# A two-buffer ring for the down phase's raw blocks, five held blocks, recurrence tiles allocated early, more gate tiles

## The chip, the cores and the metric

The kernel runs on one core of one Trainium2 chip. The metric is the device time of one execution in microseconds; the median of three runs of the kernel before is 3393.79 us (3392.86 to 3396.34).

## What is computed

One encoder layer on 1024 + 256 tokens (`x_prompt`, `x_sample`), D = 1024, feed-forward width 2816, in float32. The reference, cut to what matters:

```python
def swiglu(h, w_gate, w_up, w_down):
    return (jax.nn.silu(h @ w_gate) * (h @ w_up)) @ w_down

h = rms_norm(x, norm_g[0])
x = x + 0.5 * rms_norm(swiglu(h, ffn_w_gate[0], ...), norm_g[1])
h = rms_norm(x, norm_g[2])
p = h @ w_in
p_rw, p_att, p_gate = _split(p, [RWKV_COLS, ATT_COLS, GATE_COLS])
y_a = rwkv7_bidir(p_rw, ...)          # 8 heads x 64, both directions
y_b = axial_gqa(p_att, qk_norm_g)     # 8 query heads, 2 key heads
g_a, g_b = _split(sigmoid(p_gate + b_gate), [D_MODEL, D_MODEL])
merged = g_a * (y_a @ w_branch_a) + g_b * (y_b @ w_branch_b)
x = x + rms_norm(merged @ w_out, norm_g[3])
h = rms_norm(x, norm_g[4])
x = x + 0.5 * rms_norm(swiglu(h, ffn_w_gate[1], ...), norm_g[5])
```

## The kernel before, in words

Every operand of a float32 matmul is split into a high and a low half (`split`, L115 on ACT makes the high half, L116 on VectorE the low one), and a product is three matmuls: high by high, high by low, low by high. The stages follow one another: first feed-forward network (from the start to 878 us), projections and attention with gates, the preparation of the recurrence, the recurrence (1742 to 2296 us) with branch b between its steps, branch a, the output projection, the second feed-forward network, the end.

**Feed-forward.** `gate_up` makes 11 pairs of hidden columns. At the end of a pair it writes seven combinations of the two (`A11` to `A22`, `S1` to `S4`) to the DRAM tensor `a_d` (L360), four combinations of the down weights to `t_d` (L352). `down` then multiplies by one level of Strassen-Winograd: `DOWN` lists four banks X, Y, Z, V with 2, 1, 2 and 2 products, each over 11 blocks, so 77 blocks. A block (L393 to L404) is a load of 128x640 from `a_d` into a raw tile `sraw` (L395), its split into `S`, a load of 128x512 (`traw`, L400 or L403) from `t_d` or the weights `wd`, and its split. `mm` (L406) does the 3 matmuls for one of five token tiles, so a block is 15 matmuls. In the banks X, Y and Z, `S` is one of six slots of a tile `sr`; in bank V it is a tile `sS` of the ring `t5`, which has three buffers. The raw tiles come from the ring `x1` (two buffers) for the first two blocks and from `sc` (six buffers) after that; `sc` is also used by `gate_up` until its last column. The last `LAST` = 3 blocks of bank V are held: their matmuls are done token tile by token tile, so that tile 0 is finished while the others still run. `done` (L411) combines the banks, `half` (L377) squares and scales, `end` (L381) adds the residual and writes the row; `after` starts the next norm and, after the first network, the transposes (L176, L180, L181) which the projections (L140) read.

**Recurrence.** `loop_consts` (L685) allocates its constants and eight tiles `AR`, which are cleared before use, four on VectorE and four on POOL (L708), and two early tiles `bk0`. The pools it gets are `ep` and `cp`; `ep` lies in memory that is free during the preparation. `fetch` (L894) loads `AR` and `BK` per step, `g` (L920) multiplies them, L927 on VectorE masks the result with `gm`, POOL writes it to `Bm`, and the inverse (L959) follows.

**Branches.** `branch` (L1410) multiplies the recurrence's or the attention's output, five chunks of 256 tokens (`yr`, `yT`), by eight weight tiles (`pbr`, L1427), multiplies by a gate tile `g` loaded from `gate_d` (L1430, L1431), and, in branch a, `emit_m` adds branch b's tile `mb` (L1470, L1471) and splits the sum for the output projection (`po`, L1513). `NGA` = 6 is the number of `g` buffers in branch a, and `m` has three.

The order of the instructions on each engine is the scheduler's, by data dependences and by the buffers of the rings; all DMAs of these stages are issued from SP, whose queue is in order.

Of the kernel before, what the change touches and what calls it, by code (L numbers as in the profile page):

```python
# [7 lines left out]
F32 = mybir.dt.float32  # L8
F32R = mybir.dt.float32r
# [26 lines left out]
NH = NF // 2  # L36
TH = TT // 2
HT = NT // 2
LAST = 3

AB7 = ("A11", "A12", "S2", "S1", "S4", "S3", "A22")
DOWN = (("X", (("A11", "B11"), ("A12", "B21"))), ("Y", (("S2", "T2"),)), ("Z", (("S1", "T1"), ("S4", "B22"))),
# [7 lines left out]
class K:  # L50
# [311 lines left out]
    def down(self, W, WY, st, ps, wd, a_d, t_d, gb, xres, put, after):  # L362

        nc = self.nc

        sr = self.hp.tile([128, 6, 2, HT], F32R, name="sr", tag="h512")
        uv = self.hp.tile([128, 3, TH, 512], F32, name="uv", tag="h512")
        u, p5, v = (uv[:, i] for i in range(3))
        xr = self.hp.tile([128, 4, D], F32, name="xr", tag="h256")
        s2 = WY.tile([128, TT, 2], F32, name="s2")  # L370
        ys = [None] * TT
        lo, hi = slice(0, 512), slice(512, 1024)

        def half(t, h, src):

            hs = (lo, hi)[h]
            y = ys[t][:, hs]  # L377
            nc.scalar.activation(out=self.junk[:, :512], in_=src, func=AF.Square, accum_out=s2[:, t, h:h + 1])
            nc.vector.tensor_tensor(out=y, in0=src, in1=gb[:, hs], op=ALU.mult)

        def end(t):  # L381
            x = xr[:, t % 4]
            nc.sync.dma_start(out=x, in_=xres(t))
            ss = st.tile([128, 1], F32, name="ss")
            nc.vector.tensor_tensor(out=ss, in0=s2[:, t, 0:1], in1=s2[:, t, 1:2], op=ALU.add)
            sd = st.tile([128, 1], F32, name="sd")
            nc.scalar.activation(out=sd, in_=ss, func=AF.Sqrt, scale=4.0 / D, bias=self.eps4)
            r = st.tile([128, 1], F32, name="r")
            nc.vector.reciprocal(r, sd)
            nc.vector.scalar_tensor_tensor(out=ys[t], in0=ys[t], scalar=r, in1=x, op0=ALU.mult, op1=ALU.add)  # L390
            nc.sync.dma_start(out=put(t), in_=ys[t])

        def block(n, small, sn, tn, f):  # L393
            raw = W.tile([128, HT], F32, name="sraw", tag="x1" if n < 2 else "sc")
            nc.sync.dma_start(out=raw, in_=a_d[AB7.index(sn), f])  # L395
            S = W.tile([128, 2, HT], F32R, name="sS", tag="t5") if small else sr[:, n % 6]
            self.split(S[:, 0], S[:, 1], raw)
            raw = W.tile([128, 512], F32, name="traw", tag="w2")
            if tn[0] == "T":
                nc.sync.dma_start(out=raw, in_=t_d[int(tn[1]) - 1, f])  # L400
            else:
                fb, c = f + NH * (tn[1] == "2"), 512 * (tn[2] == "2")
                nc.sync.dma_start(out=raw, in_=wd[fb * 128:fb * 128 + 128, c:c + 512])  # L403
            return S, self.opr(raw)  # L404

        def mm(p, i, S, T, first, last):  # L406
            ts = slice(i * 128, i * 128 + 128)
            for m, (x, y) in enumerate(((0, 0), (0, 1), (1, 0))):
                nc.tensor.matmul(p, lhsT=S[:, x, ts], rhs=T[:, y], start=first and m == 0, stop=last and m == 2, skip_group_check=True)  # L409

        def done(bank, second, i, p):  # L411
            t, w = i, TH + i
            if bank == "X" and not second:
                nc.scalar.copy(u[:, i], p)
            elif bank == "X":
                ys[t] = WY.tile([128, D], F32, name="y", tag="y")
                half(t, 0, p)
            elif bank == "Y":
                nc.vector.tensor_tensor(out=u[:, i], in0=u[:, i], in1=p, op=ALU.add)
            elif bank == "Z" and not second:  # L420
                nc.scalar.copy(p5[:, i], p)
            elif bank == "Z":
                y = ys[t][:, hi]
                nc.vector.tensor_tensor(out=y, in0=u[:, i], in1=p, op=ALU.add)
                half(t, 1, y)
                end(t)
            elif not second:
                ys[w] = WY.tile([128, D], F32, name="y", tag="y")
                y = ys[w][:, hi]
                nc.vector.tensor_tensor(out=v[:, i], in0=u[:, i], in1=p, op=ALU.add)  # L430
                nc.vector.tensor_tensor(out=y, in0=v[:, i], in1=p5[:, i], op=ALU.add)
                half(w, 1, y)
            else:
                y = ys[w][:, lo]
                nc.vector.tensor_tensor(out=y, in0=u[:, i], in1=p, op=ALU.add)
                half(w, 0, y)
                end(w)
        n = 0
        for bank, prods in DOWN:
            bk = [ps.tile([128, 512], F32, name="pd", tag="mm") for _ in range(TH)]  # L440
            for j, (sn, tn) in enumerate(prods):
                final = bank == "V" and j == 1
                kept = []
                for f in range(NH):
                    S, T = block(n, bank == "V", sn, tn, f)
                    n += 1
                    if final and f >= NH - LAST:
                        kept.append((f, S, T))
                        continue
                    for i in range(TH):  # L450
                        mm(bk[i], i, S, T, j == f == 0, f == NH - 1)
                        if f == NH - 1:
                            done(bank, j, i, bk[i])

                for i in range(TH if kept else 0):
                    for f, S, T in kept:
                        mm(bk[i], i, S, T, False, f == NH - 1)
                    done(bank, j, i, bk[i])
                    after(TH + i, ys)
                if j == len(prods) - 1 - (bank == "V"):  # L460
                    after(bank, ys)
# [143 lines left out]
       "TT": 7, "tt": 9, "y1": 6, "zs": 2, "Sn": 3, "SP": 2}  # L605
RPB = {"i": 4, "g": 1, "z": 1, "s": 1}
NGD = 5
NGA = 6
WFB = {}
Y4 = 2  # L610
D4 = 8
# [9 lines left out]
class Rwkv:  # L621
# [63 lines left out]
    def loop_consts(self, ep, cp):  # L685

        nc, I, kk = self.nc, self.k.I, self.k
        self.gm = ep.tile([128, 4, 128], F32, name="gm")
        nc.sync.dma_start(out=self.gm, in_=I["c_gm"].rearrange("p (u t) -> p u t", u=4))
        self.lv = cp.tile([128, 6, 128], F32, name="lv")  # L690
        nc.sync.dma_start(out=self.lv, in_=I["c_lv"].rearrange("p (u t) -> p u t", u=6))
        self.e64 = cp.tile([128, 64], F32, name="e64")
        nc.vector.tensor_copy(self.e64[:64], kk.ident[:64, :64])
        nc.vector.tensor_copy(self.e64[64:], kk.ident[64:, 64:])
        self.Bm, self.Bl = [], []
        for i in range(self.NB):
            bm = cp.tile([128, 2, 128], F16, name=f"Bm{i}")
            bl = cp.tile([128, 2, 128], F16, name=f"Bl{i}")
            nc.gpsimd.memset(bm, 0.0)
            nc.gpsimd.memset(bl, 0.0)  # L700
            self.Bm.append(bm)
            self.Bl.append(bl)
        self.bk0 = [ep.tile([128, 4, 2, 64], F32, name=f"BK{i}") for i in range(2)]
        self.step_no = 0
        self.AR = []
        for i in range(self.NAR):
            ar = (ep if i < 2 else cp).tile([128, 4, 2, 2, 64], F32, name=f"AR{i}")
            (nc.vector if i < 4 else nc.gpsimd).memset(ar, 0.0)  # L708
            self.AR.append(ar)
        self.ar_no = 0  # L710

    def pad_tile(self, W):
# [182 lines left out]
    def fetch(self, pp, segs, W, out):  # L895

        nc, q = self.nc, pp["q"]
        for d, (sg, early) in enumerate(segs):
            cc = slice(4 * sg, 4 * sg + 4)
            AR = self.AR[self.ar_no % len(self.AR)]  # L900
            self.ar_no += 1
            for h in range(2):
                hs = slice(64 * h, 64 * h + 64)
                nc.sync.dma_start(out=AR[hs, :, h], in_=self.xs["ar"][q, d][hs, cc])
            BK = self.bk0.pop() if self.bk0 else W.tile([128, 4, 2, 64], F32, name="BK", tag="BK")
            nc.sync.dma_start(out=BK, in_=self.xs["bk"][q, d][:, cc])
            out[d] = (AR, BK)

# [393 lines left out]
def build(tc, I, O):  # L1302
    nc = tc.nc
    k = K(tc, I, O)
    with tc.tile_pool(name="cst", bufs=1) as cp, tc.tile_pool(name="dr", bufs=1, space=DRAM) as dr, \
# [14 lines left out]
        with tc.tile_pool(name="hp", bufs=1, side="right") as hp, tc.tile_pool(name="wp", bufs=2, side="right") as k.wp:  # L1320
# [3 lines left out]
            with tc.tile_pool(name="W", bufs=1, side="right") as W0, tc.tile_pool(name="ps", bufs=1, space=PSUM) as ps:  # L1324
                W, ps = Bufs(W0, FB), Bufs(ps, FP)
# [52 lines left out]
            with tc.tile_pool(name="vp", bufs=1) as vp:  # L1378
                Vt = vp.tile([128, TT, 2, 2, 64], F32R, name="Vt", tag="Vt")

                with tc.tile_pool(name="W", bufs=1) as W0, tc.tile_pool(name="ps", bufs=1, space=PSUM) as ps:
                    W = Bufs(W0, {"t5": 3, "act": 2, "pad": 3})
# [64 lines left out]
        with tc.tile_pool(name="hp", bufs=1) as hp:  # L1447
            k.hp = Bufs(hp, {"h512": 2, "h256": 1})
            mT = [k.htile(ci) for ci in range(3)]
            with right:  # L1450
# [12 lines left out]
                        pass  # L1463
                early.close()
                with tc.tile_pool(name="W", bufs=1) as W0, tc.tile_pool(name="ps", bufs=4, space=PSUM) as ps:
                    W = Bufs(W0, {"g": NGA, "m": 3})

                    def emit_m(dt, ci, c0, n, g):
                        mb = W.tile([128, n], F32, name="mb", tag="m")
# [16 lines left out]
                    first = out_w(right.enter_context(tc.tile_pool(name="wo", bufs=1, side="right")), 0)  # L1486
# [110 lines left out]
```

## Time and profile before

| what | value |
|---|---|
| median of three runs | 3393.79 us |
| profiled execution, its own time | 3395.69 us |
| its span | 3393.9 us |
| mean granted clock of TensorE | 0.986 |
| TensorE busy | 3268.3 us, 96% |
| VectorE busy | 2106.7 us, 62% |
| ACT busy | 1559.1 us, 46% |
| DMA, mean over the span | 128 GB/s |

A row of a timeline is a merged run of equal instructions: start, duration from first start to last end, engine, line, operation, tiles, count, and in brackets how long the engine stood idle before it and what released it. A row of waits names who waited for whom, the total, the number of times and the longest. A row of stretches gives busy time by engine, then TensorE's granted clock (1.00 is full speed), the share of the DMA engines and what they moved. "to landing" is the time from a DMA's issue to the arrival of its data.

### The profile page before, as it was taken

The page shows a single profiled execution, that of the slowest core. Times are in us where ns is not written, and L with a number is a line of the kernel's source. Part 1 is how long each engine was busy: PE and PEld are TensorE (multiplying, and loading weights), DVE is VectorE, ACT ScalarE, POOL GpSimd, SP SyncE. Part 2 cuts the span into 40 slices and gives each one's busy share as a digit, 9 for nine tenths or more (in the row PEclk, how much of TensorE's full clock was granted, in tenths as well). Part 3 has the DMA queues.
Part 4 walks back from the last instruction along what each step waited for, and adds up shares of the span by engine and source line. Part 5 has one row for each costly group of instructions (what it writes and reads, how often), then busy time and mean ns, then how long its engine had stood idle before and what let it go on. Part 6 is the DMA issues. An engine that isn't in the chain of part 4 may idle for free.

```text
span 3393.9 us, 57823 instructions
## 1 busy us (share of the span) xinstructions
PE 3268.3 (96%) x21750; PEld 2738.1 (81%) x21750; DVE 2106.7 (62%) x4047; ACT 1559.1 (46%) x3048; POOL 333.4 (10%) x695
## 2 busy tenths in 40 slices
PE   7999999999899999999979999998999999999998
PEld 6888888788778888887767888888777888887887
DVE  7665665456446767648867676655548656656446
ACT  6322223345325666746646666652444223233434
POOL 0000000000011000012234444420000000000000
PEclk9999999999999999999999999999999999999999
DMA  4343344756234121224353222127523433436655
GB/s 145 132 143 123 125 142 135 243 174 205 84 97 132 57 65 57 73 92 151 133 168 103 60 75 74 46 73 227 183 80 118 141 118 129 138 118 210 196 165 183
DMA packets 255640, 433.64 MB, mean 128 GB/s; under 512 B 28032, under 2 KB 109184, under 8 KB 255232
## 3 DMA queue, kind: packets, MB, share of 16 engines
q1 hardware_dynamic: 255360, 429.95, 38.9%
q8 instruction: 171, 2.80, 0.4%
q14 instruction: 109, 0.89, 0.1%
HBM read 278.97 MB, written 147.59 MB: 126 GB/s over the span
## 4 chain that ended last, share of the span: by engine, by line
PE 41%; DMA 3%; DVE 3%; ACT 1%; issue 1%; POOL 1%; SPq 0%; DVEq 0%; POOLq 0%; ACTq 0%
PE pd L409 8%; PE Z L258 4%; PE V L258 4%; PE T L258 4%; PE X L258 3%; PE po L1513 3%; PE g L920 2%; PE Y L258 2%; PE inv L959 2%; PE inv L964 2%; PE inv L965 1%; PE zu L996 1%; PE zu L1000 1%; PE zu L1007 1%; PE yp L1022 1%; PE sp L1015 1%
## 5 line engine op out<-in xcount | busy, mean ns | idle before, releaser
L140 PE MATMUL pp<-hT,whi 128*128 128x512 f32 (+1 forms) x1776 | 503.6, 363 | 8.3 <-ACT qk L1194 5.3
L115 ACT CAST op<-w 128x512 fp32r<-128x512 f32 x356 | 220.6, 623 | 513.5 <-PE V L258 122.2
L409 PE MATMUL pd<-op,sr 128*128 128x512 f32 x1650 | 384.0, 395 | 8.5 <-ACT sr L115 8.5
L409 PEld LDWEIGHTS pd<-op,sr 128*128 128x128 f32 x1650 | 312.2, 189 | 80.0 <-ACT sr L115 9.4
L116 DVE TENSOR_TENSOR op<-w,op 128x512 fp32r<-128x512 f32 x356 | 243.0, 689 | 185.1 <-ACT op L115 184.6
L140 PEld LDWEIGHTS pp<-hT,whi 128*128 128x128 f32 x1776 | 315.7, 192 | 48.0 <-ACT qk L1194 6.1
L140 PE MATMUL pp<-hT,wlo 128*128 128x512 f32 (+1 forms) x888 | 320.6, 361 | 0.0
L258 PEld LDWEIGHTS T<-hT,op 128*128 128x128 f32 x2112 | 275.3, 193 | 24.3 <-DVE op L116 10.5
L258 PE MATMUL T<-hT,op 128*128 128x256 f32 x2112 | 280.6, 286 | 10.7 <-DVE op L116 9.6
L258 PE MATMUL X<-hA,op 128*128 128x512 f32 x1056 | 263.2, 397 | 6.5 <-DVE op L116 3.3
L967 ACT CAST tt<-inv 128x512 f16<-128x512 f32 x400 | 226.3, 589 | 91.7 <-PE inv L965 69.1
L258 PEld LDWEIGHTS X<-hA,op 128*128 128x128 f32 x1056 | 196.3, 190 | 50.1 <-DVE op L116 4.4
L961 DVE TENSOR_TENSOR y<-inv,lv 128x256 f16<-128x256 f32 x400 | 162.1, 419 | 84.0 <-PE inv L959 61.0
L116 DVE TENSOR_TENSOR sr<-sraw,sr 128x640 fp32r<-128x640 f32 x110 | 90.6, 825 | 172.8 <-ACT sr L115 172.7
L140 PEld LDWEIGHTS pp<-hT,wlo 128*128 128x128 f32 x888 | 170.1, 192 | 18.7
L115 ACT CAST sr<-sraw 128x640 fp32r<-128x640 f32 x110 | 80.0, 729 | 185.5 <-PE pd L409 176.2
L409 PE MATMUL pd<-op,sS 128*128 128x512 f32 x660 | 152.2, 391 | 0.0
L1427 PE MATMUL pbr<-yT,whi 128*128 128x256 f32 x640 | 127.4, 298 | 22.9 <-ACT yT L115 8.4
L258 PE MATMUL V<-hX,op 128*128 128x512 f32 x528 | 144.7, 395 | 0.0
L409 PEld LDWEIGHTS pd<-op,sS 128*128 128x128 f32 x660 | 123.3, 188 | 25.9 <-DVE sS L116 0.6
L258 PE MATMUL Z<-hB,op 128*128 128x512 f32 x528 | 137.3, 394 | 0.0
L964 PE MATMUL inv<-y,tt 128*128 128x128 f16 x800 | 130.1, 220 | 0.0
(315 smaller groups left out, 6730.2 us busy)
## 6 DMA issues: line engine op xcount, KB each, us to landing
sraw<-a_d SPq DMA_DIRECT2D x154, 320.0 KB, 3.2
w<-wgu SPq DMA_DIRECT2D x192, 256.0 KB, 3.3
a_d<-sg SPq DMA_DIRECT2D x88, 320.0 KB, 2.6
w<-wd SPq DMA_DIRECT2D x88, 256.0 KB, 2.8
t_d<-w SPq DMA_DIRECT2D x88, 256.0 KB, 2.8
traw<-t_d SPq DMA_DIRECT2D x88, 256.0 KB, 3.1
a_d<-s SPq DMA_DIRECT2D x66, 320.0 KB, 2.3
traw<-wd SPq DMA_DIRECT2D x66, 256.0 KB, 3.6
```

The costliest lines, as they stand in the source:

```text
L115: self.nc.scalar.copy(dst_h, src)
L116: self.nc.vector.tensor_tensor(out=dst_l, in0=src, in1=dst_h.bitcast(F32), op=ALU.subtract)
L140: nc.tensor.matmul(p[:, :n], lhsT=a[:, ks], rhs=h[:, b, k], start=i == 0, stop=i == 23)
L258: self.nc.tensor.matmul(out, lhsT=o[:, a, ks], rhs=rhs(k, b), start=start and i == 0, stop=stop and i == 11, skip_group_check=True)
L409: nc.tensor.matmul(p, lhsT=S[:, x, ts], rhs=T[:, y], start=first and m == 0, stop=last and m == 2, skip_group_check=True)
L920: nc.tensor.matmul(g[:, 2 * d:2 * d + 2], lhsT=BK[:, cs[d] % 4], rhs=AR[:, cs[d] % 4], start=True, stop=True)
L959: nc.tensor.matmul(m[:, h], lhsT=Bm[:, h], rhs=tt[:, h, 0], start=True, stop=True)
L961: nc.vector.tensor_tensor(out=y1, in0=m, in1=mask(l), op=ALU.mult)
L964: nc.tensor.matmul(dbl[:, h, 0], lhsT=tt[:, h, 1], rhs=y1[:, h], start=True, stop=True)
L967: nc.scalar.copy(tt, dbl)
L1427: nc.tensor.matmul(p, lhsT=a[:, ks], rhs=ys[ci][:, b, kk], start=i == 0, stop=i == 11)
L1513: nc.tensor.matmul(p, lhsT=m[:, a, kk, mo:mo + 128], rhs=wo[hf][:, b, kk], start=i == 0, stop=i == 23)
```

## The change

Four things are done. In `down`, raw tiles of the first five blocks and of all blocks of bank V come from `x1`; the others from `sc` as before. In bank V the split block is a `t5` tile (three buffers) for odd blocks and a pair of `sc` tiles (three pairs) for even ones, and `LAST` is 5. In `loop_consts` the `AR` tiles are allocated directly behind `gm`, ahead of the other constants, and cleared at the end as before; the tiles `bk0` are gone, and all `BK` come from the ring. In branch a `g` has ten buffers and `m` five.

```diff
@@ -36,7 +36,7 @@
-LAST = 3
+LAST = 5
@@ -391,10 +391,18 @@
         def block(n, small, sn, tn, f):
-            raw = W.tile([128, HT], F32, name="sraw", tag="x1" if n < 2 else "sc")
+
+            raw = W.tile([128, HT], F32, name="sraw", tag="x1" if n < 5 or small else "sc")
             nc.sync.dma_start(out=raw, in_=a_d[AB7.index(sn), f])
-            S = W.tile([128, 2, HT], F32R, name="sS", tag="t5") if small else sr[:, n % 6]
-            self.split(S[:, 0], S[:, 1], raw)
+            if not small:
+                S = sr[:, n % 6]
+                S = (S[:, 0], S[:, 1])
+            elif n % 2:
+                S = W.tile([128, 2, HT], F32R, name="sS", tag="t5")
+                S = (S[:, 0], S[:, 1])
+            else:
+                S = [W.tile([128, HT], F32R, name="sH", tag="sc") for _ in range(2)]
+            self.split(S[0], S[1], raw)
@@ -605,7 +613,7 @@
-NGA = 6
+NGA = 10
@@ -687,6 +695,8 @@
         nc.sync.dma_start(out=self.gm, in_=I["c_gm"].rearrange("p (u t) -> p u t", u=4))
+
+        self.AR = [(ep if i < 2 else cp).tile([128, 4, 2, 2, 64], F32, name=f"AR{i}") for i in range(self.NAR)]
         self.lv = cp.tile([128, 6, 128], F32, name="lv")
@@ -700,13 +710,9 @@
-        self.bk0 = [ep.tile([128, 4, 2, 64], F32, name=f"BK{i}") for i in range(2)]
         self.step_no = 0
-        self.AR = []
-        for i in range(self.NAR):
-            ar = (ep if i < 2 else cp).tile([128, 4, 2, 2, 64], F32, name=f"AR{i}")
+        for i, ar in enumerate(self.AR):
             (nc.vector if i < 4 else nc.gpsimd).memset(ar, 0.0)
-            self.AR.append(ar)
         self.ar_no = 0
@@ -902,7 +908,7 @@
-            BK = self.bk0.pop() if self.bk0 else W.tile([128, 4, 2, 64], F32, name="BK", tag="BK")
+            BK = W.tile([128, 4, 2, 64], F32, name="BK", tag="BK")
@@ -1463,7 +1469,7 @@
-                    W = Bufs(W0, {"g": NGA, "m": 3})
+                    W = Bufs(W0, {"g": NGA, "m": 5})
```

The changed order on the engines, at three places. The first is SP at the start of the first down phase, from the second block's load on, before:

```order
L395 DMA sraw<-a_d 128x640
L403 DMA traw<-wd 128x512 x5
L360 DMA a_d<-sg 128x640 x2
L360 DMA a_d<-s_4998 128x640
L360 DMA a_d<-s_4999 128x640
L360 DMA a_d<-sg 128x640 x2
L360 DMA a_d<-s_5000 128x640
L534 DMA gb<-ng 128x1024
L395 DMA sraw<-a_d 128x640 x11
```

and now, from the third block's load on:

```order
L396 DMA sraw<-a_d 128x640
L411 DMA traw<-wd 128x512
L396 DMA sraw<-a_d 128x640
L411 DMA traw<-wd 128x512
L383 DMA xr<-x_prompt 128x1024
L360 DMA a_d<-sg 128x640 x2
L360 DMA a_d<-s_4998 128x640
L360 DMA a_d<-sg 128x640 x2
L360 DMA a_d<-s_4999 128x640
L360 DMA a_d<-s_5000 128x640
L542 DMA gb<-ng 128x1024
L396 DMA sraw<-a_d 128x640 x8
```

The loads of blocks 2 and 3 and one `xr` now stand ahead of the seven writes of the last column and of `gb`; block 4's is the first behind them.

The second is VectorE at the entry to the recurrence, from the low half of branch b's first weight tile on, before:

```order
L113 SCALAR_TENSOR_TENSOR wlo<-wraw,whi 128x512
L693 COPY e_15945<-ident 64x64
L694 COPY e_15945<-ident 64x64
L708 MEMSET AR_15978 128x1024
L708 MEMSET AR_15980 128x1024
L708 MEMSET AR_15982 128x1024
L708 MEMSET AR_15984 128x1024
L116 TENSOR_TENSOR yT<-yr,yT 128x1024
L1431 SCALAR_TENSOR_TENSOR g<-g,pbr 128x256
L927 TENSOR_TENSOR gs<-g,gm 128x512
```

and now:

```order
L113 SCALAR_TENSOR_TENSOR wlo<-wraw,whi 128x512
L703 COPY e_15964<-ident 64x64
L704 COPY e_15964<-ident 64x64
L715 MEMSET AR_15956 128x1024
L715 MEMSET AR_15957 128x1024
L116 TENSOR_TENSOR yT<-yr,yT 128x1024
L933 TENSOR_TENSOR gs<-g,gm 128x512
```

Two of the four clears have moved ahead, among the preparation's operations, and the mask of the first `g` product comes before the first gate product.

The third is SP in branch a, from the fourth of its five loads of `yr` on (the numbers tell buffers apart), before:

```order
L1416 DMA yr_26630<-ya_d_75 128x4x256
L1430 DMA g_26652<-gate_d_71 128x256
L1416 DMA yr_26635<-ya_d_75 128x4x256
L1470 DMA mb_26655<-mb_d_74 128x256
L1430 DMA g_26673<-gate_d_71 128x256
L1470 DMA mb_26676<-mb_d_74 128x256
L1430 DMA g_26694<-gate_d_71 128x256
L1470 DMA mb_26697<-mb_d_74 128x256
L1430 DMA g_26715<-gate_d_71 128x256
L1470 DMA mb_26718<-mb_d_74 128x256
L1430 DMA g_26736<-gate_d_71 128x256
L124 DMA wraw_26747<-wba 128x512
```

and now:

```order
L1422 DMA yr_26641<-ya_d_75 128x4x256
L124 DMA wraw_26758<-wba 128x512
L1422 DMA yr_26646<-ya_d_75 128x4x256
L1436 DMA g_26663<-gate_d_71 128x256
L1476 DMA mb_26666<-mb_d_74 128x256
L1436 DMA g_26684<-gate_d_71 128x256
```

The second weight tile's load has moved from behind five gate loads to ahead of the fifth `yr`, and the first gate load from ahead of the fifth `yr` to behind it.

## Rows read from the trace of the kernel before

**Rows 1.** The page: busy time by engine.

```profile
PE 3268.3 (96%) x21750; PEld 2738.1 (81%) x21750; DVE 2106.7 (62%) x4047; ACT 1559.1 (46%) x3048; POOL 333.4 (10%) x695
```

**Rows 2.** Timeline of PE, start of the first and the second down phase.

```profile
601.42 7.00 PE L409 MATMUL pd<-op,sr 128*128 128x512 f32 x30
612.83 7.36 PE L409 MATMUL pd<-op,sr 128*128 128x512 f32 x25 [4.41 <-ACT sr L115]
...
3121.57 8.65 PE L409 MATMUL pd<-op,sr 128*128 128x512 f32 x30 [4.13 <-ACT sr L115]
```

**Rows 3.** Timeline of all engines from 604 us, first down phase.

```profile
603.97 0.82 DVE L358 TENSOR_TENSOR s<-sg,s 128x640 f32<-128x640 f32 x1
604.82 0.32 SPq L360 DMA_DIRECT2D a_d<-s  x1
...
605.70 11.58 SPq L395 DMA_DIRECT2D sraw<-a_d  x11
...
612.05 4.03 ACT L115 CAST sr<-sraw 128x640 fp32r<-128x640 f32 x5 [2.98 <-DMA sraw<-a_d]
```

**Rows 4.** The tile sraw, 593 to 620 us: low-half split, time to landing.

```profile
L116 DVE TENSOR_TENSOR sr<-sraw,sr x7: 817/826/826, 612.8 to 620.0; 128x640 fp32r<-128x640 f32 x7
...
DMA to landing us min/median/max: 3.3/6.3/7.1
```

**Rows 5.** Busy time and clock of three stretches behind waits: columns as described above.

```profile
612.83:615.83 3.00, 3.00 (x7) 2.42 (x8) 2.97 (x4) 2.67 (x4) 0.00 (x0) 0.51 0.96 346
...
3121.57:3124.57 3.00, 3.00 (x7) 2.42 (x8) 2.99 (x4) 2.65 (x4) 0.00 (x0) 0.50 0.93 328
...
2351.20:2355.00 3.80, 3.80 (x18) 3.80 (x19) 1.75 (x5) 0.57 (x2) 0.00 (x0) 0.50 0.78 227
```

**Rows 6.** The tile sraw, 780 to 870 us (bank V): time to landing.

```profile
DMA to landing us min/median/max: 2.8/3.5/5.3
```

**Rows 7.** Timelines of DVE and PE, end of the first down phase.

```profile
872.23 1.28 DVE L390 SCALAR_TENSOR_TENSOR y<-y,r,xr 128x1024 f32<-128x1024 f32 x1
...
877.05 1.28 DVE L390 SCALAR_TENSOR_TENSOR y<-y,r,xr 128x1024 f32<-128x1024 f32 x1
...
876.72 1.40 PE L409 MATMUL pd<-op,sS 128*128 128x512 f32 x5
...
906.72 0.73 PE L140 MATMUL pp<-hT,whi 128*128 128x512 f32 x2 [1.08 <-DVE hT L181]
```

**Rows 8.** Timelines of PE and DVE, end of the kernel.

```profile
3361.68 22.76 PE L409 MATMUL pd<-op,sS 128*128 128x512 f32 x99
...
3389.14 1.28 DVE L390 SCALAR_TENSOR_TENSOR y<-y,r,xr 128x1024 f32<-128x1024 f32 x1
```

**Rows 9.** Waits of PE, 1730 to 1760 us.

```profile
PE pbr L1427 <- ACT yT L115: 7.2, 1, 7.2
PE inv L959 <- DVE tt L955: 3.7, 2, 1.9
PE pbr L1427 <- DVE yT L116: 3.2, 1, 3.2
```

**Rows 10.** Timelines of DVE and SP, entry to the recurrence.

```profile
1739.79 0.91 DVE L708 MEMSET AR<- 128x1024 f32 x1 [0.26 <-issue]
...
1743.96 1.22 DVE L116 TENSOR_TENSOR yT<-yr,yT 128x1024 fp32r<-128x1024 f32 x1
...
1740.73 1.25 SPq L904 DMA_DIRECT2D AR<-ar_d  x2
```

**Rows 11.** Waits of PE and of DVE in branch a and around it.

```profile
PE pbr L1427 <- DVE g L1431: 5.2, 5, 2.4
PE po L1513 <- DVE g L1431: 3.1, 1, 3.1
PE pbr L1427 <- ACT whi L112: 2.5, 1, 2.5
...
DVE g L1431 <- DMA g<-gate_d: 16.7, 13, 3.4
```

More of the change, by code (lines that the diff above doesn't have):

```diff
@@ L408, in mm @@
             for m, (x, y) in enumerate(((0, 0), (0, 1), (1, 0))):
-                nc.tensor.matmul(p, lhsT=S[:, x, ts], rhs=T[:, y], start=first and m == 0, stop=last and m == 2, skip_group_check=True)
+                nc.tensor.matmul(p, lhsT=S[x][:, ts], rhs=T[:, y], start=first and m == 0, stop=last and m == 2, skip_group_check=True)
         def done(bank, second, i, p):
```

## Prediction

> **What bounds the kernel now.** I read the page first, for the engines' shares; then TensorE's own timeline, for the places where it stands still; then, at each of them, the waits and the queue of the engine that releases it; and the table by stretches, for the clock after each. TensorE is busy for 3268.3 us of a span of 3393.9 us [rows 1], so the path is TensorE nearly everywhere, and only its idle time and the time in which it runs at half clock can be won. The change takes no matmul away and adds none. Its five parts touch five places; each is costed against the profiled execution, whose time (3395.69 us) is 1.9 us above the median of the runs shown (3393.79 us). I take the same saving off the median.
>
> **Start of each down phase.** Down is 77 blocks of 15 matmuls. TensorE runs two of them, 30 matmuls in 7.00 us (with the overlap of neighbours some 3.4 us a block), then stands still for 4.41 us in the first feed-forward network and for 4.13 us in the second, waiting for the ACT half of block 2's split [rows 2]. The reader should see why that is late: block 2's load is on SP behind the writes of the last feed-forward column and the broadcast of `gb`; the last of those writes waits for a VectorE operation of 0.82 us, and the load itself is issued at 605.70 only [rows 3]. Loads issued there take 6.3 us to land, 7.1 at most [rows 4]: 605.70 and 6.3 is 612.0, ACT's split starts at 612.05 [rows 3] and TensorE at 612.83 [rows 2].
> The gap costs more than its length. In the 3.0 us behind it the granted clock is 0.51 in one phase and 0.50 in the other, the level of 1.2 GHz, and 7 matmuls are done [rows 5]. At the rate of rows 2 (30 in 7.00 us, 0.23 us each) they would need 1.6 us: 1.4 us lost. Together 4.41 + 4.13 + 2 x 1.4 = 11.3 us.
> The Trainium skill ("TensorE: Matmul & The Clock Gate", "Loop structure matters more than you think") states as a rule that a long wait for a transfer between matmuls leaves TensorE at the lower clock when it goes on. By that rule the gaps alone, 8.5 us, would be too little, and the trace agrees [rows 5].
> With the change blocks 0 to 3 are loaded ahead of these writes, since ring `x1` gives a buffer back when a block is split. Two more splits of 0.82 us on VectorE [rows 4] come ahead of the operations that the writes wait for, so the writes and `gb` go out 1.6 us later: block 4's load is issued near 607.3, lands near 613.6, and ACT's split (five in 4.03 us, 0.8 us each [rows 3]) ends near 614.4. TensorE, without its gap, wants block 4 at 601.42 + 4 x 3.4 = 615.0. VectorE's half is needed two matmuls later (615.5) and ends near 615.3. It just fits; with a landing of 7.1 us it is late by some 0.7 us. I take 0.3 us a phase: **10.7 us**, with bounds 7.3 (2 us late in each, the clock kept) and 11.3. The two extra splits hide beside TensorE's first blocks; the load of `xr` that moves ahead of the writes is one of the transfers that land beside those two blocks.
> A page would price the landing otherwise: the Trainium skill ("DMA: Bandwidth & Descriptors", "Anatomy of one DMA") fits 2.0 us and the bytes at 436 GB/s, measured on another issuing path, which makes 2.75 us for 320 KB. By that estimate block 4 comes 3.6 us earlier and the term would be the full 11.3; rows 4 say 6.3 in this place, and go into the sum.
>
> **Five blocks held, six buffers for them.** In the last product the five held blocks are run tile by tile: 15 matmuls a tile instead of 9, 3.4 us instead of 2.04. The first tile is done at P - 13.6 instead of P - 8.2, P being the end of the phase on TensorE. No matmul moves in or out.
> After the first phase a chain follows (VectorE, ACT, VectorE, for each tile: combine, square, scale, root, residual, then the next norm). Its residual additions come 4.8 us apart (872.23, 877.05) though TensorE gives a tile each 2.04, so TensorE waits for it, and the projections start at 906.72, 28.6 us after P = 876.72 + 1.40 = 878.1 [rows 7]. An earlier first tile moves this chain earlier by up to 5.4 us. But in the new order VectorE also takes splits of weights and the copies of the next transposes between the tiles, and the tiles now come at 3.4 us each, 13.6 us for the last four. Laid out by hand with the durations of rows 7 the projections start at P + 27, so I take **2.0 us**, from -1 (the transposes, which TensorE takes in order, wait for a tile between the held matmuls) to +6.
> At the end of the kernel the five tiles go one after the other on VectorE, from P - 13.6, with an estimated 4.1 us each: 1.28 for the addition [rows 8], 0.7 each for combining, squaring and scaling, which are half as large, and 0.7 for the root's three small steps; the fourth and fifth end at P + 1.4 and P + 5.6. Before, the last addition ended at 3390.42, 6.0 us after P = 3384.44 [rows 8]. **0.3 us**, 0 to 0.6.
>
> **Entry to the recurrence.** TensorE waits 7.2 us for the high half of `yT` and then 3.2 us for the low one [rows 9]. The first wait is for loads of weights and `yr`, which stay. The second is VectorE's: four clears of `AR`, from 1739.79 on, stand ahead of that split at 1743.96, 1.04 us each [rows 10]. Two of them move into the preparation, so the split starts 2.1 us earlier. SP also drops five loads of some 0.6 us from the train that ends with the `BK`s [rows 10], and the first `g` products come ahead of most of the `pbr` products, which then fill two waits for `tt` of 3.7 us together [rows 9]. From 2.1 (the clears alone) to 5.8 (both waits filled too). I take **3.5 us**, nearer the middle, since the chain through POOL between them stays. The two clears in the preparation take some 2 us of VectorE there while TensorE works; if that cover is gone they cost 0.5 at most. The low clock behind the first wait stays.
>
> **Branch a.** TensorE waits there 5.2 us for the products with `g` and 2.5 us for `whi` [rows 11], and runs at half clock behind the latter [rows 5]. The new order issues the second weight tile ahead of the fifth `yr`, which removes the 2.5 us and, with it, about 1.9 us of low clock (half of the 3.8 us [rows 5]). Against this: the first `g` and `mb` now go behind the last `yr`, and VectorE has a backlog at the branch's end: `po` waits 3.1 us for it [rows 11]. Ten buffers let loads run ahead, but they don't make VectorE faster. I take **2.5 us**, from -1 (the late `g` costs what the weights give) to +6 (most of both waits).
>
> **Sum.** 10.7 + 2.0 + 0.3 + 3.5 + 2.5 = 19.0 us, so 3375 us from the median of 3393.79. With all lower bounds the saving is 7.3 - 1 + 0 + 2.1 - 1 = 7.4 us (3386), with all upper ones 11.3 + 6 + 0.6 + 5.8 + 6 = 29.7 us (3364).
>
> **Rivals.**
> *The gap moves to block 4.* If SP stands at block 2's load until block 0 is split, the writes behind it are late by more than the two splits. At 3 us late, block 4 is a new gap of 3 us with its 1.4 us of low clock: the starts give 11.3 - 8.8 = 2.5, the whole 10.8, the time 3383 us. For it: VectorE is in order, and busy with the writes' operands [rows 3]. Against it: blocks 0 and 1 were split without stopping the queue, since TensorE had them at 601.42.
> *The chains shift whole.* The transition gives 5.4 us and branch a loses all its waits, 6 us: 26 us, 3368 us. For it: the wait on `gate_d` is VectorE's longest, 16.7 us [rows 11]. Against it: the wait of `po`, which is VectorE's work and no load's.
> *Two raw buffers starve the last bank (slower).* The 22 blocks of bank V load through a ring of two instead of six. A slot turns in the landing plus 1.6 us of splits plus 0.3 of issue, so a block can come every (landing + 1.9) / 2: at 3.5 us, the median there [rows 6], 2.7 us, less than the 3.4 of a block. It decides above 4.9 us of landing for many blocks in a row. If the 6.3 us of rows 4 held there, 4.1 us a block, 0.7 late, times 44 blocks is 31 us, and with 19 saved the time is 3406 us. Against it: the median, and the six buffers for splits.
>
> **How the numbers follow.** A measurement of this kernel tells 0.2%, 6.8 us, from no change. The forecast has 0.70, the gap at block 4 0.12, the whole shift 0.10, the starved bank 0.03; 0.05 is left for parts that cancel, near 3390. The range is 3364 to 3388 us: all bounds of the unknown costs, the first two rivals, and 2 us for the last case. Faster by over 0.2% comes from the forecast but for its edge and from the first two rivals: 0.88; same 0.08; slower 0.04.
>
> **What would show it.** In the new profile: 75 matmuls without a stop from the start of each down phase and a clock of 1.00 there; block 4's split by ACT just before TensorE comes to it; the first tile of the last product 13.6 us before the phase's end, projections some 27 us after it; the low half of `yT` two clears earlier and the first `g` product soon behind; no wait for `whi` in branch a. Wrong would be: a stop at block 4 or 5 of more than 2 us, waits for `sS` or `sH` through bank V, or a longer wait of `po`.

## The result and the profile after

The changed kernel takes 3375.28 us (median of four runs, 3374.04 to 3376.69) against 3394.53 us: a ratio of 0.9943, 95% interval 0.9926 to 0.9961. That is 19.2 us less; 19.0 was forecast. The profiled execution has a span of 3373.8 us. Two later sets of runs gave 0.9940 (0.9925 to 0.9955) and 0.9943 (0.9929 to 0.9956).

The page of the changed kernel, by engine (before: [rows 1]):

```profile
PE 3268.5 (97%) x21750; PEld 2742.1 (81%) x21750; DVE 2101.1 (62%) x4047; ACT 1556.8 (46%) x3048; POOL 332.1 (10%) x695
```

TensorE's work is the same; what went is time in which it stood still or ran at half clock. The starts of the two down phases, TensorE's timeline of the changed kernel (before: [rows 2]):

```profile
598.78 26.50 PE L417 MATMUL pd<-op,sr 128*128 128x512 f32 x116
...
3104.70 25.46 PE L417 MATMUL pd<-op,sr 128*128 128x512 f32 x108
```

and the busy time and clock of both starts, with the columns of [rows 5]:

```profile
600.00:616.00 16.00, 16.00 (x72) 13.27 (x71) 10.01 (x16) 6.46 (x11) 0.00 (x0) 1.00 1.00 334
...
3110.00:3125.00 15.00, 15.00 (x66) 12.08 (x65) 9.50 (x15) 7.93 (x13) 0.00 (x0) 1.00 1.00 359
```

The row of each start is whole, no bracket interrupts it, and the clock is 1.00 where it was 0.51 and 0.50. Why it is whole, in the queue of SP and in ACT's timeline of the changed kernel:

```profile
594.18 0.33 SPq L396 DMA_DIRECT2D sraw<-a_d  x1
...
597.79 0.80 SPq L360 DMA_DIRECT2D a_d<-sg  x2
...
604.01 0.40 SPq L542 DMA_DIRECT2D gb<-ng  x1
604.46 8.91 SPq L396 DMA_DIRECT2D sraw<-a_d  x8
...
610.10 0.73 ACT L115 CAST sr<-sraw 128x640 fp32r<-128x640 f32 x1 [3.65 <-DMA sraw<-a_d]
```

Block 3's load is issued at 594.18, ahead of the first write at 597.79. Block 4's follows `gb` at 604.46 and its data release ACT at 610.10, 5.6 us later; TensorE, which began at 598.78, comes to it 13.6 us after that, at 612.4. So 1.6 us are to spare after ACT's 0.73. In the second phase of the same profile the margin is smaller:

```profile
3101.92 4.53 SPq L396 DMA_DIRECT2D sraw<-a_d  x7
...
3107.92 0.73 ACT L115 CAST sr<-sraw 128x640 fp32r<-128x640 f32 x1 [4.74 <-DMA sraw<-a_d]
```

There the load takes 6.0 us, and TensorE comes to block 4 at 3109.39, 0.7 us after the end of ACT's split. Over the sixteen starts of the eight profiles with this edit, the load of block 4 took 5.2 to 7.1 us and the margin was 0.6 to 2.3 us; TensorE stopped at block 4 in none.

The transition behind the first phase (before: [rows 7]), timelines of VectorE and TensorE of the changed kernel:

```profile
857.54 1.28 DVE L390 SCALAR_TENSOR_TENSOR y<-y,r,xr 128x1024 f32<-128x1024 f32 x1
...
862.51 1.28 DVE L390 SCALAR_TENSOR_TENSOR y<-y,r,xr 128x1024 f32<-128x1024 f32 x1
...
867.34 1.28 DVE L390 SCALAR_TENSOR_TENSOR y<-y,r,xr 128x1024 f32<-128x1024 f32 x1
...
873.83 1.28 DVE L390 SCALAR_TENSOR_TENSOR y<-y,r,xr 128x1024 f32<-128x1024 f32 x1
...
883.01 1.28 DVE L390 SCALAR_TENSOR_TENSOR y<-y,r,xr 128x1024 f32<-128x1024 f32 x1
...
886.55 1.23 PE L176 MATMUL ptr<-dg,y 128*128 128x128 f32 x4 [3.10 <-ACT dg L166]
...
895.70 0.84 PE L140 MATMUL pp<-hT,whi 128*128 128x512 f32 x2 [1.08 <-DVE hT L181]
```

Three tiles come 4.9 us apart; the fourth and the fifth are 6.5 and 9.2 us behind, because the copies of transposes (L181) and the split of a weight tile stand between them on VectorE. TensorE's last matmul of the phase ends at 870.01, so the projections start 25.7 us behind it, before 28.6.

The end of the kernel (before: [rows 8]), where TensorE's last matmul ends at 3364.61; VectorE's last addition ends at 3370.29, 5.7 us later:

```profile
3369.01 1.28 DVE L390 SCALAR_TENSOR_TENSOR y<-y,r,xr 128x1024 f32<-128x1024 f32 x1
```

TensorE's waits at the entry to the recurrence (before: [rows 9]):

```profile
PE pbr L1433 <- ACT yT L115: 7.8, 1, 7.8
PE inv L965 <- DVE tt L961: 3.5, 2, 1.9
PE g L926 <- DMA AR<-ar_d: 1.3, 1, 1.3
PE pbr L1433 <- DVE yT L116: 0.9, 1, 0.9
```

and in branch a, from the recurrence's last `inv` on (before: [rows 11], whose rows of TensorE start some 58 us later):

```profile
PE pbr L1433 <- DVE g L1437: 5.4, 6, 1.6
PE po L1519 <- DVE g L1437: 3.3, 1, 3.3
PE pbr L1433 <- ACT yT L115: 2.0, 1, 2.0
PE pbr L1433 <- DVE yT L116: 1.8, 3, 0.9
PE pbr L1433 <- ACT whi L112: 0.8, 1, 0.8
```

In the kernel before, over the same stretch, the first of these rows was

```profile
PE pbr L1427 <- DVE g L1431: 7.1, 7, 2.4
```

At the entry the wait for the low half fell from 3.2 to 0.9 us, one wait of 1.3 us for an `AR` load is new, and the two waits for `tt` are nearly as they were, 3.5 us where 3.7 was. In branch a the wait for `whi` is 0.8 instead of 2.5 us, that for `g` 5.4 instead of 7.1, and the one of `po` is as it was.

### The profile page after: what moved, and what is told of

It is laid out like the page before. It is cut to its first block, busy times and chain, and to the rows that moved or that the text cites. A ratio compares the mean times of both kernels' runs of the same rounds, so it can differ in the third digit from the quotient of the medians.

```text
span 3373.8 us, 57809 instructions
## 1 busy us (share of the span) xinstructions
PE 3268.5 (97%) x21750; PEld 2742.1 (81%) x21750; DVE 2101.1 (62%) x4047; ACT 1556.8 (46%) x3048; POOL 332.1 (10%) x695
## 5 line engine op out<-in xcount | busy, mean ns | idle before, releaser
L258 PEld LDWEIGHTS T<-hT,op 128*128 128x128 f32 x2112 | 274.9, 192 | 24.1 <-DVE op L116 10.5
L258 PE MATMUL T<-hT,op 128*128 128x256 f32 x2112 | 280.0, 286 | 10.7 <-DVE op L116 9.7
L258 PE MATMUL X<-hA,op 128*128 128x512 f32 x1056 | 263.3, 397 | 6.5 <-ACT op L115 3.3
L258 PEld LDWEIGHTS X<-hA,op 128*128 128x128 f32 x1056 | 196.3, 190 | 50.0 <-DVE op L116 4.3
L258 PE MATMUL V<-hX,op 128*128 128x512 f32 x528 | 144.8, 396 | 0.0
L258 PE MATMUL Z<-hB,op 128*128 128x512 f32 x528 | 137.3, 395 | 0.0
L971 PE MATMUL inv<-tt,y 128*128 128x128 f16 x800 | 128.8, 219 | 0.0
L116 DVE TENSOR_TENSOR op<-traw,op 128x512 fp32r<-128x512 f32 x154 | 105.5, 686 | 36.8 <-ACT op L115 36.7
```

The source lines that it names most:

```text
L116: self.nc.vector.tensor_tensor(out=dst_l, in0=src, in1=dst_h.bitcast(F32), op=ALU.subtract)
L258: self.nc.tensor.matmul(out, lhsT=o[:, a, ks], rhs=rhs(k, b), start=start and i == 0, stop=stop and i == 11, skip_group_check=True)
L971: nc.tensor.matmul(dbl[:, h, 1], lhsT=y1[:, h], rhs=tt[:, h, 1], start=True, stop=True)
```

## The experiments

Two profiles of one execution each differ also where nothing was changed: the first product of bank Z (L258) starts at 69.40 us in the profile of before and at 66.89 us in that of after, with the same instructions up to there. So twelve more runs were made, and the stretches of fourteen profiles are set side by side. Each number is the difference of two instants of TensorE's timeline: *S1* and *S2* from the first to the 76th matmul of a down phase, *transition* from the 801st matmul of the first one to the first projection, *entry* from the last matmul of the preparation to the first `inv`, *branch a* from the recurrence's last `inv` to the branches' last product, with the granted clock of that stretch, *tail* from the end of the last matmul to the end of VectorE's last addition.

| profile | S1 | S2 | transition | entry | branch a (clock) | tail |
|---|---|---|---|---|---|---|
| before | 23.13 | 23.33 | 117.84 | 19.38 | 143.74 (0.95) | 5.98 |
| unedited | 24.39 | 23.36 | 117.86 | 19.62 | 138.58 (0.99) | 5.98 |
| starts | 17.04 | 17.57 | 117.85 | 19.18 | 142.38 (0.96) | 5.98 |
| three | 21.61 | 19.64 | 117.84 | 20.73 | 142.53 (0.96) | 5.98 |
| held | 25.09 | 26.45 | 117.43 | 21.72 | 142.17 (0.96) | 5.40 |
| down | 17.04 | 17.57 | 115.16 | 19.68 | 137.85 (0.98) | 5.41 |
| early | 23.38 | 23.64 | 117.85 | 16.97 | 138.15 (0.96) | 5.98 |
| gates | 24.45 | 23.44 | 117.87 | 19.82 | 137.87 (0.99) | 5.98 |
| after | 17.04 | 17.57 | 115.54 | 17.53 | 140.82 (0.96) | 5.68 |
| again | 17.04 | 17.56 | 115.79 | 16.06 | 137.34 (0.99) | 5.70 |
| again_5 | 17.04 | 17.56 | 117.23 | 16.54 | 136.88 (0.98) | 5.69 |
| last3 | 17.04 | 17.56 | 118.15 | 16.17 | 137.88 (0.99) | 6.30 |
| last6 | 17.04 | 17.57 | 113.24 | 16.18 | 137.52 (0.99) | 4.18 |
| last6_5 | 17.04 | 17.56 | 113.25 | 17.02 | 139.72 (0.95) | 4.18 |

### The raw ring for the first blocks alone: `starts`

```diff
-            raw = W.tile([128, HT], F32, name="sraw", tag="x1" if n < 2 else "sc")
+            raw = W.tile([128, HT], F32, name="sraw", tag="x1" if n < 5 else "sc")
```

> The kernel before with one edit: the raw tiles of blocks 0 to 4 come from x1 (before: 0 and 1). Theory: both stops of TensorE at block 2 (4.41 and 4.13 us) go, and with each the 3.0 us at half clock behind it (1.4 us), so TensorE runs 75 matmuls without a stop and the kernel gains 11.3 us, up to 11.9. Rival, the low clock comes anyway: 8.5 us. Rival, the gap only moves to block 4: 2.5 to 5 us. Nothing else moves by more than 1 us, but where the clock falls by chance.

Measured: 3381.89 us against 3391.9 us, ratio 0.9970 (0.9959 to 0.9980). S1 falls from 23.13 to 17.04 and S2 from 23.33 to 17.57: 6.1 and 5.8 us, the stops and the low clock behind them. No stop at block 4. The theory holds, at its upper figure. Without the edit S1 scatters: in the profiles `unedited` and `gates` it is 24.4 us, with stops of 4.2 and 4.3 us, since the low clock behind the stop lasted longer there. In the kernel before the clock was 1.00 again from 615.83 us, 3.0 us behind the stop; in `unedited` the second 3 us behind it were at 0.50 too:

```profile
613.82:616.82 3.00, 3.00 (x8) 2.32 (x8) 1.12 (x2) 0.27 (x1) 0.00 (x0) 0.50 0.92 294
```

Over the four profiles with unedited starts (`before`, `unedited`, `early`, `gates`) S1 and S2 are 23.8 and 23.4 us on average, so that the edit is worth 12.7 us by this mean and 11.9 by the first profile.

### One block fewer: `three`

```diff
-            raw = W.tile([128, HT], F32, name="sraw", tag="x1" if n < 2 else "sc")
+            raw = W.tile([128, HT], F32, name="sraw", tag="x1" if n < 3 else "sc")
```

> The kernel before with raw tiles of blocks 0 to 2 from x1 (before: 0 and 1), blocks 3 and 4 from sc as before. It tells whether the place of a block's load among the writes sets the stop. Theory: the stop moves to block 3, the first behind the writes; its load is issued 0.8 us later than block 2's was (one more split ahead of the writes), lands near 612.8, its ACT half ends near 613.6 where TensorE wants it at 611.6: a stop of 2 us in each phase; 75 matmuls take 19 us (before 23.1 and 23.3, with the change 17.0 and 17.6), 20.5 if the clock falls behind it. Rival, the loads of sc go early once x1 has moved: no stop, 17.0 and 17.6.

Measured: 3387.29 us against 3392.62 us, ratio 0.9985 (0.9976 to 0.9994). The starts in TensorE's timeline of this kernel:

```profile
600.42 10.40 PE L409 MATMUL pd<-op,sr 128*128 128x512 f32 x45
613.47 11.90 PE L409 MATMUL pd<-op,sr 128*128 128x512 f32 x44 [2.64 <-ACT sr L115]
...
3108.92 10.70 PE L409 MATMUL pd<-op,sr 128*128 128x512 f32 x45
3121.43 8.93 PE L409 MATMUL pd<-op,sr 128*128 128x512 f32 x37 [1.81 <-ACT sr L115]
```

Three blocks, 45 matmuls, run, and the stop is at block 3, 2.64 and 1.81 us where 2 was expected. So the stop belongs to the first block whose load stands behind the writes, and each block moved ahead takes some 2 us off it. The stretches behind the two stops, with the clock as the third number from the end:

```profile
615.00:618.00 3.00, 3.00 (x9) 2.31 (x8) 2.81 (x4) 1.60 (x3) 0.00 (x0) 0.50 0.77 218
...
3121.50:3124.50 3.00, 3.00 (x13) 2.45 (x14) 3.00 (x5) 2.92 (x5) 0.00 (x0) 1.00 0.94 346
```

Behind the longer stop the clock fell to 0.50, behind the shorter it stayed at 1.00: 21.61 and 19.64 us for the same 75 matmuls. The 19 us expected for a kept clock were near; the 20.5 for a fallen one were 1.1 us too few.

### Bank V's rings and five held blocks alone: `held`

```diff
-LAST = 3
+LAST = 5
-            raw = W.tile([128, HT], F32, name="sraw", tag="x1" if n < 2 else "sc")
+            raw = W.tile([128, HT], F32, name="sraw", tag="x1" if n < 2 or small else "sc")
...
+            elif n % 2:
+                S = W.tile([128, 2, HT], F32R, name="sS", tag="t5")
...
+                S = [W.tile([128, HT], F32R, name="sH", tag="sc") for _ in range(2)]
```

> The kernel before with the edit of bank V alone: raw tiles of bank V from x1, split blocks in three t5 tiles and three pairs of sc tiles, five blocks held; blocks 2 to 4 stay in sc. Theory: the stops at block 2 stay (4.3 us, or up to 1.5 us longer in each phase, since SP now issues two loads of bank V ahead of the writes); the projections start 25 to 26 us after the first down phase's last matmul, not 28.6, so 2.5 to 3 us there and 0.3 us at the end; in all between 3 us faster and no change. Rival, two raw buffers starve bank V: waits for sS or sH of 0.5 us and more per block, up to 20 us slower.

Measured: 3395.07 us against 3391.9 us, ratio 1.0010 (1.0001 to 1.0019). Slower, outside what was expected. TensorE's timeline of this kernel at the two starts:

```profile
613.12 17.14 PE L417 MATMUL pd<-op,sr 128*128 128x512 f32 x63 [5.19 <-ACT sr L115]
...
3123.88 16.40 PE L417 MATMUL pd<-op,sr 128*128 128x512 f32 x62 [7.01 <-ACT sr L115]
```

The stops at block 2 grew to 5.19 and 7.01 us. The reason stands in the queue of SP and in ACT's timeline of this kernel:

```profile
591.39 0.33 SPq L396 DMA_DIRECT2D sraw<-a_d  x1
...
594.59 0.73 ACT L115 CAST sS<-sraw 128x640 fp32r<-128x640 f32 x1 [2.17 <-DMA sraw<-a_d]
...
596.21 0.33 SPq L396 DMA_DIRECT2D sraw<-a_d  x1
...
606.50 3.34 SPq L396 DMA_DIRECT2D sraw<-a_d  x6
```

SP now has two loads of bank V, needed 200 us later, ahead of the writes, since `x1` is free and bank V is its next user; the first of them is split into an `sS` tile at 594.59 already, while block 2's load goes out at 606.50. The stops are 0.8 and 2.9 us longer than in the kernel before, where up to 1.5 was expected. S1 and S2 are 2.0 and 3.1 us longer than in the first profile of before; of S1's, up to 1.3 us are within the scatter of the unedited starts. No wait for `sS` or `sH` shows in bank V in this run or in the changed kernel, so two raw buffers don't starve it.

### Both edits of the down phase: `down`

```diff
-            raw = W.tile([128, HT], F32, name="sraw", tag="x1" if n < 2 or small else "sc")
+            raw = W.tile([128, HT], F32, name="sraw", tag="x1" if n < 5 or small else "sc")
```

The diff is against `held`.

> The kernel before with both edits of the down phase (raw tiles of blocks 0 to 4 and of bank V from x1, six slots, five held), without the recurrence's and branch a's. Theory: blocks 2 to 4 now take x1 ahead of bank V's first two, so the loss of the run 'held' at the starts (2.0 and 3.1 us) is gone: 11.8 us at the starts, 2.3 us or more at the transition, 0.3 at the end, in all 14 to 16 us faster. Rival, the parts add: 10.0 us faster and 3.2 us slower make 6.8 us faster.

Measured: 3379.29 us against 3393.76 us, ratio 0.9954 (0.9938 to 0.9969): 14.5 us. The parts don't add, 10.0 less 3.2 would be 6.8. With blocks 2 to 4 as `x1`'s next users, bank V's first loads no longer go out ahead of the writes (the first split into `sS` is at 644.27 us, in `held` it was at 594.59), and S1 and S2 are 17.04 and 17.57.

### Three and six held blocks: `last3`, `last6`

```diff
-LAST = 5
+LAST = 3
```

> The changed kernel with three blocks held instead of five, all else as in it. Theory: the first tile of the last product is done 8.2 us before the phase's end on TensorE, not 13.6, and the projections start 28 to 29 us after that end, not 25.7: 2 to 3 us slower than the changed kernel in the first phase and 0.3 us at the end. Rival, the gain at the transition is that of the six slots: same as the changed kernel.

Measured: 3374.84 us against 3393.76 us, ratio 0.9945 (0.9930 to 0.9960). The transition takes 118.15 us, with five held blocks 115.2 to 117.4 (five profiles), and the tail 6.30 instead of 5.7. So the transition's gain is that of the held blocks, not of the six slots. By the time alone, 1.7 us above the changed kernel beside it (3373.11), the two are not told apart.

```diff
-LAST = 5
+LAST = 6
```

> The changed kernel with six blocks held, which fill all six slots. Theory: the chain behind the last product takes 4.8 us a tile and TensorE 4.1 us instead of 3.4, so the first tile is done 16.3 us before the end and the projections start up to 2.7 us earlier relative to it: 1 to 3 us faster than the changed kernel. Rival, the last held block's split waits for a slot and TensorE for it, 1 to 2 us in each phase: slower than the changed kernel.

Measured: 3369.27 us against 3393.76 us, ratio 0.9930 (0.9914 to 0.9947), the changed kernel beside it 3373.11. The transition takes 113.24 us, the tail 4.18. TensorE's timeline of this kernel, behind the first down phase, which ends at 874.04:

```profile
877.84 3.35 PE L176 MATMUL ptr<-dg,y 128*128 128x128 f32 x16 [3.80 <-DVE hT L181]
...
895.79 0.73 PE L140 MATMUL pp<-hT,whi 128*128 128x512 f32 x2 [1.08 <-DVE hT L181]
```

Four tiles are finished while TensorE still multiplies, and the projections start 21.7 us behind it. Part of this is a shift: more transposes (L176), and short waits, now lie between the held matmuls, so that the phase itself ends later (91.5 us from its 801st matmul to its end, 89.2 before). The transition counts both, and it is 2 to 4 us shorter than with five held blocks. With more runs:

> The changed kernel with six blocks held, again, with more runs beside the changed kernel: 3 to 4 us faster than it, of which 2.4 at the transition and 1.5 at the end; rival, the difference was scatter: within 1 us of it.

Measured: 3370.52 us, ratio 0.9930 (0.9917 to 0.9942), the changed kernel beside it 3373.84. So it is 3.8 and 3.3 us below the changed kernel in the medians, and its transition and tail were the shortest in both profiles; the intervals of the ratios overlap, though in the second set every run of it is below every run of the changed kernel. It is the fastest version found.

### The recurrence's constants alone: `early`

```diff
+        self.AR = [(ep if i < 2 else cp).tile([128, 4, 2, 2, 64], F32, name=f"AR{i}") for i in range(self.NAR)]
         self.lv = cp.tile([128, 6, 128], F32, name="lv")
...
-        self.bk0 = [ep.tile([128, 4, 2, 64], F32, name=f"BK{i}") for i in range(2)]
...
-            BK = self.bk0.pop() if self.bk0 else W.tile([128, 4, 2, 64], F32, name="BK", tag="BK")
+            BK = W.tile([128, 4, 2, 64], F32, name="BK", tag="BK")
```

> The kernel before with the edit of the recurrence's constants alone (AR allocated behind gm, no early BK). Theory now: 1.9 us, as in the changed kernel from the last matmul of the preparation to the end of the recurrence, since the first g product waits for an AR load that SP now issues behind two BK loads; rival, the sum's term: 3.5 us, and the smaller gain in the changed kernel is chance of the clock there.

Measured: 3388.87 us against 3391.9 us, ratio 0.9991 (0.9982 to 1.0000). The theory was too low: the entry takes 16.06 to 17.53 us in the seven profiles with this edit (mean 16.6) and 19.18 to 21.72 in the seven without (mean 20.0), 3.4 us. To the end of the recurrence, the stretch that the theory named, the means differ by 3.1 us, and the 1.9 of the first pair of profiles (1.95 in this kernel) was a low draw. TensorE's waits there in this kernel:

```profile
PE pbr L1424 <- ACT yT L115: 7.8, 1, 7.8
PE inv L956 <- DVE tt L952: 3.0, 2, 1.9
PE g L917 <- DMA AR<-ar_d: 1.1, 1, 1.1
PE pbr L1424 <- DVE yT L116: 0.7, 1, 0.7
```

The wait for the low half is 0.7 us where it was 3.2, and 1.1 us come back as a wait for an `AR` load, which SP now issues behind two `BK`s. Over the seven profiles with the edit that wait is 0 to 1.3 us, and two of them have none.

### The buffers of branch a alone: `gates`

```diff
-NGA = 6
+NGA = 10
...
-                    W = Bufs(W0, {"g": NGA, "m": 3})
+                    W = Bufs(W0, {"g": NGA, "m": 5})
```

> The kernel before with ten g and five m buffers in branch a alone. Theory: the wait for the second weight tile (2.5 us) and the low clock behind it go, 2.5 to 3 us from the end of the recurrence to the last product of branch a. Rival, VectorE bounds the branch and the loads of g are only late by more: no change, or 1 us slower.

Measured: 3390.34 us against 3391.9 us, ratio 0.9995 (0.9986 to 1.0004): not told from no change by the time. The stretch takes 136.88 to 140.82 us in the seven profiles with the buffers (mean 138.3) and 137.85 to 143.74 in the seven without (mean 140.8). The wait for `whi` is 0.7 to 1.8 us with them (mean 1.2) and 1.0 to 2.5 without (mean 2.1); it doesn't go.

### The scatter: `again`, `again_5`, `unedited`

The changed kernel twice and the kernel before once more, without an edit.

> The changed kernel once more, unedited, for the scatter of the stretches in a profile: the first 70 us, the stretch behind the projections' first wait, and branch a. Theory: these three differ from the first profile of the change by 1 to 3 us each, with equal instructions, since after a stop the clock falls or doesn't; the down phases, the transition and the entry to the recurrence agree within 0.5 us. Time: 17 to 19 us below the kernel before on this chip.

Measured: 3373.11 us against 3393.76 us, ratio 0.9940: 20.7 us below, where 17 to 19 was expected. Branch a differs by 3.5 us from the first profile of the change and the first product of bank Z by 0.9. The down phases and the transition agree within 0.5 us; the entry does not, 16.06 us where 17.53 was.

> The changed kernel with more runs: 0.994 of the kernel before, 19 to 20 us.

Measured: 3373.84 us against 3392.62 us, ratio 0.9943.

> The kernel before once more, for a second profile: the down phases' first 75 matmuls take 23.1 and 23.3 us again, the projections start 28.6 us behind the first phase, the entry to the recurrence takes 19.2 to 19.9 us. Branch a took 143.7 us from the recurrence's last product in the first profile and 137.9 to 142.4 in three kernels with the same code there. Theory: it is scatter, and the new profile lies anywhere from 138 to 144 us. Rival, the unedited code always takes 142 us or more, and the shorter ones come from the other edits.

Measured: one run, 3386.67 us; branch a takes 138.58 us, with the code that took 143.74 in the first profile. So it is scatter, as the theory had it, and the longer times mostly go with the lower clock (`early` took 138.15 us at 0.96). Branch a in the second profile of before and in the second of the change, columns as above:

```profile
2258.93:2397.51 138.58, 126.74 (x1047) 121.83 (x1046) 84.31 (x210) 39.70 (x83) 4.86 (x7) 0.99 0.74 227
```

```profile
2252.17:2389.51 137.34, 126.73 (x1051) 122.13 (x1049) 83.70 (x208) 39.30 (x82) 4.84 (x7) 0.99 0.74 229
```

At a clock of 0.98 or 0.99 the stretch takes 138.2 us without the buffers (2 profiles) and 137.5 with them (5); at 0.95 or 0.96 it takes 141.8 (5) and 140.3 (2). By these small groups the buffers are worth 0.7 to 1.5 us at an equal clock; that the clock fell in five of seven profiles without them and in two of seven with them makes up the rest of the 2.5 us. Whether they keep the clock up or whether that was chance, these runs don't settle. The transition of the changed kernel scatters in the same way: 25.7 us from the phase's end to the projections at a clock of 0.87 in the first profile, 27.5 in the third, with this row:

```profile
872.00:899.00 27.00, 17.29 (x86) 14.73 (x87) 15.23 (x30) 14.27 (x30) 0.36 (x9) 0.75 0.41 147
```

## Why the prediction was right

The sum held because most of its terms did. Each was measured by itself, but only the starts, and both edits of the down phase together, are told by the time of their own runs; the entry and branch a rest on means of profiles:

| term | forecast | measured | from |
|---|---|---|---|
| starts of the down phases | 10.7 | 11.9 (12.7 by the mean of four) | S1 and S2 of before and `starts` |
| transition | 2.0 | 0.4 to 2.7, mean 1.6 | before less after, `again`, `again_5`, `down`, `held` |
| end | 0.3 | 0.3 | tail |
| entry to the recurrence | 3.5 | 3.4 | means of seven profiles each |
| branch a | 2.5 | 2.5 | means of seven profiles each |
| sum | 19.0 | 19.7; by the medians 19.2 | |

**Starts.** The mechanism was right: the stops went, and the low clock behind them. The size was too small, and the measured term lies above its upper bound of 11.3. What the low clock costs was put at 1.4 us a phase; beyond the stops, 1.7 and 1.6 us went in the first pair of profiles, and in `unedited` and `gates` the first phase's cost 3.1. The 0.3 us a phase for block 4 was too much: the block came in time in all sixteen starts, by 0.6 to 2.3 us where 0.6 was worked out. By the Trainium skill's price of a transfer ("DMA: Bandwidth & Descriptors", "Anatomy of one DMA"), 2.75 us as an estimate, the term was to be 11.3, nearer to what was measured; but it missed the landing, which took 5.2 to 7.1 us.

**Held blocks.** The laid-out P + 27 was 25.5 to 27.5. It stands for 1.6 us against the 28.6 of before, not for the 2.0 written, and 1.6 is the mean measured. The chain is still the limit, and starting it earlier by one more held block (`last6`) pays at least as much again, so more of the bound was reachable. At the end of the kernel the number was right, but the working does not give it: five tiles of 4.1 us from P - 13.6 end at P + 6.9, not at the P + 5.6 written. In the profile the additions end 9.1, 5.1 and 0.9 us before P and 1.6 and 5.7 behind it. Not in the sum: bank V of the second phase, from its 801st matmul to the end, takes 81.2 to 81.9 us in the three profiles of the change and 81.0 before, with a wait of up to 0.7 us for `uv` on VectorE.

**Entry.** The term was right, the way in part. The clears gave less than their 2.1: the two waits for `yT` together are 10.5 us on average without the edit and 8.6 with it, 1.9 less. Of the waits for `tt` only the first shrank, by 0.7 us on average; the second is 1.8 to 1.9 us in all fourteen profiles. A wait of 0.6 us for the copy `BKt`, in all seven profiles without the edit and in none with it, went too, and the wait for an `AR` load came where I had seen only fewer loads.

**Branch a.** Here the step failed and the number came out by luck. I let the wait for `whi` go; it only shrank, by some 0.9 us on average. All waits of TensorE in the stretch together are 1.6 us shorter; the rest goes with how often the clock fell. The two groups of seven profiles overlap (136.9 to 140.8 us and 137.9 to 143.7), and the run of this edit alone is not told from no change, so the 2.5 us are not shown.

**Rivals.** The gap at block 4 didn't come, and `three` shows the same mechanism one block earlier. Bank V wasn't starved by two raw buffers. But that ring did have a way to be slower, and it wasn't my rival: alone, the edit lets bank V's first loads take the queue ahead of block 2, which makes the two stops 3.7 us longer together and the starts 4 to 5 us. In the change the first edit hides what the second would cost.

## What to carry to other kernels

A tile taken from a free ring is loaded as soon as a buffer is there, whenever its user comes: giving a ring to a late stage can put that stage's loads ahead of urgent ones, and giving the ring's next turns to the urgent ones mends it. Price a stop of TensorE by the stretch up to where it is back at its old pace, not by the gap. And compare stretches over several profiles before a few microseconds are put down to an edit; an unchanged stretch is the control.

## What was not expected of the hardware

With the same instructions, one execution to the next, a stop was followed by half clock or not: a stop of 3.29 us at 1003 us in the profile of before was followed by 1.00, one of 3.63 us at the same place in the changed kernel by 0.69 over the next 3.1 us. In branch a the profiles at the lower mean clock are 2.8 to 3.6 us longer, and in the first 70 us the same point lies at 66.4 to 69.4 us over the fourteen profiles, while the starts of the down phases, without a stop, agree to 0.01 us in eight profiles.
